# Loading the y tiles of the second output product the way the first product's are loaded, and queueing its weight loads behind them

## The chip, the cores and the metric

The kernel runs on one core of a Trainium2 chip. The metric is the device time of one launch in microseconds (us). Lower is better. The engines are PE (TensorE matmul; its weight loads are shown as PEld), DVE (VectorE), ACT (ScalarE), POOL (GpSimd) and SP (SyncE, which here issues every DMA).

## The reference

One encoder layer is applied to a prompt of 1024 tokens and a sample of 256 tokens, each with 16 meta tokens in front:

```
u = rms_norm(h, norm_w) @ w_in                     # 2048 -> 6656 columns
qa, ka, va, za, qb, kb, vb, zb = split(u)
ya = global_gqa(rope(norm(qa)), rope(norm(ka)), va) * silu(za)              # 8 heads
yb = neighbourhood_attention(norm(qb), norm(kb), vb, rpb) * silu(zb)        # 8 heads
y  = concat([ya, yb]) @ w_out                      # 2048 x 2048
return h + y                                       # without the meta tokens
```

All of it is float32. `neighbourhood_attention` lets each token see a window of 8 rows x 16 columns of a grid that is 64 wide, and the meta tokens.

## The kernel before

A float32 product is made of three matmuls. `split` (L61, L62) writes a rounded copy of a tile with ACT and the remainder with DVE (names ending in `h` and `l`), and PE multiplies h*h, h*l and l*h.

The program has three parts. Two chunks project the tokens strip by strip (`strips`, L210 to L212; tiles `wh`, `wl`, `x`, `xb`, results in `pp`). Attention for the eight global and then the eight windowed heads (called local heads here) is worked into the second chunk. Each local head has four blocks (`attend_strip`): scores on PE (L438 from `qfull` and `kfull`, and L272/L273 from `q` and `km`), maxima and sums with DVE, ACT and POOL (L284, L301), the product with the values (L467, L470 into `po`), and a result `y` that is stored into the DRAM tile `yd` (L319). `yd0` holds the eight global heads and `yd1` the eight local ones. Seven of the local heads run beside the projection; the four blocks of the last one are left for the output product. That head's `qfull` comes by DRAM: the last projection of q is normalized (L237), stored into `q2d` in two pieces (L240), loaded again (L790) and split into `q` (ACT L61, DVE L62).

The output product `outproj` is seven half-size products instead of eight, taken in the order 1, 2, 5, 6, 7, 3, 4, which are called passes here. A pass has five y tiles `t` of 128 tokens from each half, and two column halves `b`, so 10 steps; a step is 24 matmuls into one PSUM tile `pq` (L949 to L951). Steps are numbered n = 0 to 69, y tiles m = n // 2. Pass 1 multiplies `yd0` with w_out rows 0 to 1023, the second pass (number 2) `yd1` with rows 1024 to 2047; both make the same output columns. A pass has 16 weight tiles: `ww` is loaded (L926, L924) into the buffers that held `xb`, and split into `wm`. During the last tile of a pass the weights of the next are split. The four remaining local blocks are woven into steps 3 to 6 by `next(self.blocks)`.

Before the change, `y_load` fills tiles of the pool tag `wl` directly (4 buffers, two for each y tile, one per half of the heads) as long as `self.yr` is None, that is, for pass 1 and for the first tile of pass 2. After `end_attention` has opened the pool `yr` (4 buffers of 512 KB), each later tile of pass 2 is one load into `yr`, which is split from there.

Up to step 10 a scheduler orders the instructions of each engine at build time, by priority (mostly the order in which the program is written) and by its own estimate of when things are ready. From step 10 on, `in_order` chains each engine's instructions in the order written. On the chip each engine then runs its list in that order: an instruction that waits holds up everything behind it on that engine, and a waiting DMA holds up all later DMAs on SP.

Of the kernel before, what the change touches and what calls it, by code (L numbers as in the profile page):

```python
# [12 lines left out]
F32 = mybir.dt.float32  # L13
# [31 lines left out]
WCH = 4  # L45
LAG = 6
TH = (NP + NS) // 2
NT = TH // P
# [6 lines left out]
class Kern:  # L55
# [824 lines left out]
    def y_load(self, p, t):  # L880

        def half(i, h):
            r = self.yr.tile([P, 8, P], F32, tag="yr", name="yr")
            self.nc.sync.dma_start(r[:], self.yd[i][:, NT * h + t])
            return r[:]

        if self.yr is None:
            los = [self.w.tile([P, WCH, P], F32R, tag="wl", name="yl") for _ in range(2)]
            for i, l in enumerate(los):
                self.nc.sync.dma_start(l[:].bitcast(F32), self.yd[p > 1][:, t, WCH * i:WCH * i + WCH])  # L890
            return los
        return [half(*x) for x in {7: [(0, 0), (0, 1)], 5: [(0, 1), (1, 1)], 6: [(0, 0)], 3: [(1, 0)], 2: [(1, 0)], 4: [(1, 1)]}[p]]

    def y_operand(self, p, t, r):
        nc = self.nc
        if len(r[0].shape) == 3 and r[0].shape[1] == WCH:
            his, los, full = [], r, [l[:].bitcast(F32) for l in r]
            for l, f in zip(los, full):
                his.append(self.w.tile([P, WCH, P], F32R, tag="wh", name="yh"))
                self.split(his[-1][:], l[:], f)  # L900
            return his, los
        if p in (2, 4):
            v = r[0]
        elif p == 7:
            v = r[0]
            nc.vector.tensor_tensor(out=v, in0=v, in1=r[1], op=ALU.subtract)
        else:
            v = self.ysum[t][:]
            a, b, op = {5: (r[0], r[-1], ALU.add), 6: (v, r[0], ALU.subtract), 3: (r[0], v, ALU.subtract)}[p]
            nc.vector.tensor_tensor(out=v, in0=a, in1=b, op=op)  # L910
        his, los = [], []
        for i in range(2):
            his.append(self.w.tile([P, WCH, P], F32R, tag="wh", name="yh"))
            los.append(self.w.tile([P, WCH, P], F32R, tag="wl", name="yl"))
            self.split(his[i][:], los[i][:], v[:, WCH * i:WCH * i + WCH])
        return his, los
# [69 lines left out]
        self.nc.sync.dma_start(self.io["y"][:, NT * h + t, FH * c + FB * b:][:, :FB], o[:])  # L986

    def outproj(self, end_attention):
        self.U, self.V, self.yr = {}, {}, None
        order = (1, 2, 5, 6, 7, 3, 4)  # L990
        N = 2 * NT * len(order)

        def step(n):
            q, r = divmod(n, 2 * NT)
            return order[q], *divmod(r, 2)

        def tile_of(m):
            return order[m // NT], m % NT

        M = NT * len(order)  # L1000
        yr, ys, wr, ws, x, out = {}, {}, {}, {}, {}, {}

        def load_y(m):
            if m < M and m not in yr:
                yr[m] = self.y_load(*tile_of(m))

        def make_y(m):
            if m < M:
                load_y(m)
                ys[m] = self.y_operand(*tile_of(m), yr.pop(m))  # L1010

        def load_w(q, j):
            if q < len(order):
                wr[q, j] = self.w_load(order[q], j)

        def make_w(q, j):
            if q < len(order):
                ws[q, j] = self.w_operand(wr.pop((q, j)))

        make_y(0)  # L1020
        for j in range(16):
            load_w(0, j)
            make_w(0, j)
        traced = None
        for n in range(N):
            p, t, b = step(n)
            q, m = n // (2 * NT), n // 2
            if n == 2 * NT - 1:
                for _ in self.blocks:
                    pass  # L1030
            if n == 2 * NT:
                end_attention()
                traced = len(self.nc.cur_bb.bb.instructions)
                load_y(m + 1)
            if n - 2 in out:
                self.store(out.pop(n - 2), *step(n - 2))
            last = t == NT - 1
            if NT - 3 <= t < NT - 1:
                for j in range(4):
                    load_w(q + 1, 8 * (t - NT + 3) + 4 * b + j)  # L1040
            if q:
                for i in (n, n + 1, n + 2):
                    if i < N and i not in x:
                        x[i] = self.x_load(*step(i))
                load_y(m + 2)
            if b == 0 and (q or not last):
                make_y(m + 1)
            if q == 0 and last and b == 1:
                make_y(m + 1)
            ps = self.products([ws[q, 8 * b + k] for k in range(8)], ys[m])  # L1050
            if last:
                for k in range(8):
                    make_w(q + 1, 8 * b + k)
            o = self.out_sums(p, 2 * t + b, ps, x.pop(n, None))
            if o:
                out[n] = o
            if 2 < n < 2 * NT:
                next(self.blocks, None)
            if traced:
                traced = self.in_order(traced)  # L1060
        for n in sorted(out):
            self.store(out[n], *step(n))
# [158 lines left out]
```

## Time and profile before

| | |
|---|---|
| median of 3 runs | 2186.74 us (2185.39 to 2188.92) |
| the profiled execution: its time | 2186.82 us |
| the profiled execution: its span | 2185.0 us |
| mean granted PE clock | 0.996 |
| PE busy | 2158.3 us (99%) |
| DVE, ACT, POOL busy | 1642.2, 1120.7, 519.3 us |
| DMA | 383.83 MB, mean 176 GB/s |

Times in the profile count from the first instruction. A row of the timeline gives the start, the duration, the engine, line, operation and tiles, and in brackets how long the engine was idle before it and what ended that idle time. A matmul's duration is longer than the distance to the next, because matmuls are pipelined; what a matmul costs is that distance. "to landing" of a DMA is the time from its issue until its semaphore says that it is complete.

### The profile page before, as it was taken

The page shows a single profiled execution, that of the slowest core. Times are in us where ns is not written, and L with a number is a line of the kernel's source. Part 1 is how long each engine was busy: PE and PEld are TensorE (multiplying, and loading weights), DVE is VectorE, ACT ScalarE, POOL GpSimd, SP SyncE. Part 2 cuts the span into 40 slices and gives each one's busy share as a digit, 9 for nine tenths or more (in the row PEclk, how much of TensorE's full clock was granted, in tenths as well). Part 3 has the DMA queues.
Part 4 walks back from the last instruction along what each step waited for, and adds up shares of the span by engine and source line. Part 5 has one row for each costly group of instructions (what it writes and reads, how often), then busy time and mean ns, then how long its engine had stood idle before and what let it go on. Part 6 is the DMA issues. An engine that isn't in the chain of part 4 may idle for free.

```text
span 2185.0 us, 34137 instructions
## 1 busy us (share of the span) xinstructions
PE 2158.3 (99%) x11736; PEld 1882.2 (86%) x11736; DVE 1642.2 (75%) x2991; ACT 1120.7 (51%) x2294; POOL 519.3 (24%) x249
## 2 busy tenths in 40 slices
PE   8999999999999999999999999999999999999999
PEld 7888888888888999998999999898989878788887
DVE  7687976787864889996799989777767677545763
ACT  6556544555544666665666666444444454232230
POOL 1232421222211233231133225333223222000000
PEclk9999999999999999999999999999999999999999
DMA  8767899988554333334233334653433471763663
GB/s 295 225 197 229 278 302 313 349 269 263 169 185 142 106 105 110 116 112 143 93 114 109 104 121 158 185 157 132 134 113 123 125 267 37 258 222 110 227 226 106
DMA packets 263038, 383.83 MB, mean 176 GB/s; under 512 B 44976, under 2 KB 113232, under 8 KB 262864
## 3 DMA queue, kind: packets, MB, share of 16 engines
q1 hardware_dynamic: 262864, 381.65, 53.5%
q8 instruction: 92, 1.51, 0.3%
q14 instruction: 82, 0.67, 0.1%
HBM read 281.01 MB, written 100.38 MB: 175 GB/s over the span
## 4 chain that ended last, share of the span: by engine, by line
PE 92%; DVE 3%; DMA 2%; ACT 1%; SPq 1%; issue 1%; POOL 0%; DVEq 0%; ACTq 0%; POOLq 0%
PE pp L210 20%; PE pp L212 20%; PE pp L211 20%; PE pq L949 6%; PE pq L951 6%; PE pq L950 6%; PE sp L438 2%; PE po L470 2%; PE sp L334 1%; PE sp L333 1%; PE sp L332 1%; PE po L372 1%; PE po L373 1%; PE po L374 1%; SPq L227 0%
## 5 line engine op out<-in xcount | busy, mean ns | idle before, releaser
L210 PE MATMUL pp<-x,wh 128*128 128x512 f32 (+1 forms) x1664 | 654.1, 394 | 7.0 <-ACT wh L61 6.5
L212 PE MATMUL pp<-x,wl 128*128 128x512 f32 (+1 forms) x1664 | 649.4, 391 | 0.2 <-DVE wl L62 0.2
L211 PE MATMUL pp<-x,wh 128*128 128x512 f32 (+1 forms) x1664 | 649.4, 391 | 0.0
L210 PEld LDWEIGHTS pp<-x,wh 128*128 128x128 f32 x1664 | 313.3, 188 | 63.7 <-ACT wh L61 7.7
L212 PEld LDWEIGHTS pp<-x,wl 128*128 128x128 f32 x1664 | 313.0, 188 | 62.4 <-DVE wl L62 1.4
L211 PEld LDWEIGHTS pp<-x,wh 128*128 128x128 f32 x1664 | 313.5, 188 | 52.1
L220 POOL PARTITION_ALL_REDUCE m<-ms x78 | 231.8, 2971 | 366.0 <-ACT ms L218 308.1
L62 DVE TENSOR_TENSOR wl<-wr,wh 128x512 fp32r<-128x512 f32 (+1 forms) x290 | 216.5, 749 | 134.0 <-ACT wh L61 109.1
L301 POOL PARTITION_ALL_REDUCE tot<-a x80 | 171.8, 2148 | 487.4 <-DVE a L299 471.2
L61 ACT CAST wh<-wr 128x512 fp32r<-128x512 f32 (+1 forms) x290 | 175.0, 607 | 207.9 <-PE pp L211 185.0
L211 PE MATMUL pp<-xb,wh 128*128 128x272 f32 x832 | 241.8, 291 | 0.0
L210 PE MATMUL pp<-xb,wh 128*128 128x272 f32 x832 | 240.4, 289 | 0.0
L212 PE MATMUL pp<-xb,wl 128*128 128x272 f32 x832 | 239.8, 288 | 0.0
L949 PE MATMUL pq<-wm,yh 128*128 128x512 f32 x560 | 221.1, 395 | 10.1 <-ACT yh L61 5.1
L950 PE MATMUL pq<-wm,yh 128*128 128x512 f32 x560 | 219.7, 392 | 0.0
L951 PE MATMUL pq<-wm,yl 128*128 128x512 f32 x560 | 219.7, 392 | 0.0
L284 POOL PARTITION_ALL_REDUCE ma<-m x80 | 107.2, 1339 | 439.1 <-DVE m L282 427.6
L210 PEld LDWEIGHTS pp<-xb,wh 128*128 128x128 f32 x832 | 157.0, 189 | 7.3
L211 PEld LDWEIGHTS pp<-xb,wh 128*128 128x128 f32 x832 | 156.9, 189 | 7.2
L212 PEld LDWEIGHTS pp<-xb,wl 128*128 128x128 f32 x832 | 157.8, 190 | 0.1
L949 PEld LDWEIGHTS pq<-wm,yh 128*128 128x128 f32 x560 | 106.2, 190 | 32.5 <-ACT yh L61 5.6
L951 PEld LDWEIGHTS pq<-wm,yl 128*128 128x128 f32 x560 | 106.1, 189 | 22.5 <-DVE yl L62 0.2
(207 smaller groups left out, 3838.5 us busy)
## 6 DMA issues: line engine op xcount, KB each, us to landing
wr<-in_w_in SPq DMA_DIRECT2D x414, 256.0 KB, 3.4
wld<-wl SPq DMA_DIRECT2D x132, 256.0 KB, 4.3
wl<-wld SPq DMA_DIRECT2D x132, 256.0 KB, 3.1
yr<-yd SPq DMA_DIRECT2D x39, 512.0 KB, 5.0
wq<-in_w_out SPq DMA_DIRECT2D x64, 256.0 KB, 5.3
td<-wq SPq DMA_DIRECT2D x64, 256.0 KB, 4.4
ww<-td SPq DMA_DIRECT2D x64, 256.0 KB, 5.7
ww<-in_w_out SPq DMA_DIRECT2D x48, 256.0 KB, 5.3
```

The costliest lines, as they stand in the source:

```text
L61: self.hi = nc.scalar.copy(hi, full).ins
L62: return nc.vector.tensor_tensor(out=lo, in0=full, in1=hi.bitcast(F32), op=ALU.subtract).ins
L210: nc.tensor.matmul(p[:, :n], wh[:, k, :], xh[:, :n], start=first, stop=False)
L211: nc.tensor.matmul(p[:, :n], wh[:, k, :], xl[:, :n], start=False, stop=False)
L212: nc.tensor.matmul(p[:, :n], wl[:, k, :], xh[:, :n], start=False, stop=last)
L220: nc.gpsimd.partition_all_reduce(m2[:], ms[:], P, RED.add)
L284: nc.gpsimd.partition_all_reduce(ma[:], m1[:], P, RED.max)
L301: nc.gpsimd.partition_all_reduce(tot[:], a1[:], P, RED.add)
L438: nc.tensor.matmul(dst, k[:, o:o + P], qfv[:, a:e, :], start=True, stop=True)
L949: nc.tensor.matmul(ps[:], yh, wh, start=k == 0, stop=False)
L950: nc.tensor.matmul(ps[:], yh, wl, start=False, stop=False)
L951: nc.tensor.matmul(ps[:], yl, wh, start=False, stop=k == 7)
```

## The change

The second pass is loaded like the first: two loads of 256 KB into `wl` tiles for every y tile (`p in (1, 2)`), with no `yr` tile. In passes 1 and 2 the load of tile m+1 stands in the program at the first step of tile m (b = 0) and its split at the second (b = 1). Before, pass 1 had both at b = 0 (at b = 1 for its last tile), and pass 2 loaded two tiles ahead and split at b = 0. From pass 5 on it is as before, except that the first tile of pass 5 (m = 10) is now loaded where it is split. The loads of the next pass's weights are chained on SP behind the latest direct y load (`issue_after(self.lasty)`). At the start of `outproj` all loads of pass 1 are written ahead of all splits, with the load of the second y tile ahead of the last four weights.

```
     def y_load(self, p, t):
...
-        if self.yr is None:
+        if p in (1, 2):
             los = [self.w.tile([P, WCH, P], F32R, tag="wl", name="yl") for _ in range(2)]
             for i, l in enumerate(los):
-                self.nc.sync.dma_start(l[:].bitcast(F32), self.yd[p > 1][:, t, WCH * i:WCH * i + WCH])
+                self.lasty = self.nc.sync.dma_start(l[:].bitcast(F32), self.yd[p - 1][:, t, WCH * i:WCH * i + WCH]).ins
             return los
...
     def outproj(self, end_attention):
...
+        load_y(0)
+        for j in range(16):
+            if j == 12:
+                load_y(1)
+            load_w(0, j)
         make_y(0)
         for j in range(16):
-            load_w(0, j)
             make_w(0, j)
...
             if n == 2 * NT:
                 end_attention()
                 traced = len(self.nc.cur_bb.bb.instructions)
-                load_y(m + 1)
...
             if NT - 3 <= t < NT - 1:
-                for j in range(4):
-                    load_w(q + 1, 8 * (t - NT + 3) + 4 * b + j)
+                with self.tc.issue_after(self.lasty):
+                    for j in range(4):
+                        load_w(q + 1, 8 * (t - NT + 3) + 4 * b + j)
...
+            direct = m + 1 < 2 * NT
+            if direct:
+                (load_y, make_y)[b](m + 1)
+            elif m + 2 < M:
                 load_y(m + 2)
-            if b == 0 and (q or not last):
-                make_y(m + 1)
-            if q == 0 and last and b == 1:
+            if b == 0 and not direct:
                 make_y(m + 1)
```

The number of instructions is the same on PE, DVE and ACT. Their order differs only from the start of the output product until the second pass, and on SP also before pass 5. Three places follow.

PE where step 0 begins, before: `sp_20203` and `sp_20204` are the scores of the block ahead of the last head's four, `pq_20386` is step 0.

```order
L438 MATMUL sp_20203<-qfull_19454,kfull_19438 128x128 x2
L272 MATMUL sp_20203<-q_19457,km_19442 112x256
L273 MATMUL sp_20203<-q_19457,km_19442 112x256
L438 MATMUL sp_20204<-qfull_19454,kfull_19438 128x192 x2
L949 MATMUL pq_20386<-wm_20298,yh_20290 128x512
L950 MATMUL pq_20386<-wm_20298,yh_20290 128x512
L951 MATMUL pq_20386<-wm_20298,yl_20286 128x512
```

The same place after the change; `qfull_20270`, `kfull_20254` and `q_20273` belong to the last local head, `pq_20380` is step 0.

```order
L438 MATMUL sp_20203<-qfull_19454,kfull_19438 128x128 x2
L272 MATMUL sp_20203<-q_19457,km_19442 112x256
L273 MATMUL sp_20203<-q_19457,km_19442 112x256
L438 MATMUL sp_20204<-qfull_19454,kfull_19438 128x192 x2
L438 MATMUL sp_20504<-qfull_20270,kfull_20254 128x128 x2
L438 MATMUL sp_20505<-qfull_20270,kfull_20254 128x192 x2
L272 MATMUL sp_20504<-q_20273,km_20258 112x256
L273 MATMUL sp_20504<-q_20273,km_20258 112x256
L949 MATMUL pq_20380<-wm_20332,yh_20326 128x512
```

The scores of the last head's first block stood at the end of step 3; they now stand ahead of step 0.

SP around the last head's q, before: `q2d15` is that head's q in DRAM, `ww` here are weights of pass 2.

```order
L926 DMA ww_20741<-in_w_out 128x512
L240 DMA q2d15_164<-rs_r0_20001 128x272
L926 DMA ww_20743<-in_w_out 128x512
L926 DMA ww_20833<-in_w_out 128x512
L478 DMA bt_20268<-in_bt 128x1152
L926 DMA ww_20835<-in_w_out 128x512
L926 DMA ww_20837<-in_w_out 128x512
L926 DMA ww_20839<-in_w_out 128x512
L319 DMA yd1_166<-y_20055 128x4x64
L773 DMA zd15_138<-zt_20181 128x512
L790 DMA qfull_20270<-q2d15_164 128x784
```

The same place after the change; `yl_20315` is the second half of y tile 1.

```order
L890 DMA yl_20315<-yd0_165 128x512
L778 DMA kfull_20254<-kfd9_78 128x240
L779 DMA kfull_20254<-k2d9_148 128x784
L780 DMA kfull_20254<-kfd9_78 128x16
L789 DMA qfull_20270<-qfd15_122 128x240
L240 DMA q2d15_164<-rs_r0_20001 128x272
L790 DMA qfull_20270<-q2d15_164 128x784
L478 DMA bt_20268<-in_bt 128x1152
```

The 16 weight loads of pass 2 are gone from this stretch (they now come between the y loads of tiles 2 to 5), and the load of q follows its store at once.

SP at the end of the last block, before: `y_20829` is that block's result, `yr_21009` the second y tile of pass 2.

```order
L319 DMA yd1_166<-y_20733 128x4x64
L319 DMA yd1_166<-y_20829 128x4x64
L884 DMA yr_21009<-yd1_166 128x1024
L940 DMA o_21011<-in_xr 128x512
L940 DMA o_21013<-in_xr 128x512
L940 DMA o_21015<-in_xr 128x512
L884 DMA yr_21017<-yd1_166 128x1024
```

The same place after the change; `y_20823` is the last block's result, `yl_21015` and `yl_21016` are the halves of the second y tile of pass 2.

```order
L319 DMA yd1_166<-y_20733 128x4x64
L319 DMA yd1_166<-y_20823 128x4x64
L940 DMA o_21009<-in_xr 128x512
L940 DMA o_21011<-in_xr 128x512
L940 DMA o_21013<-in_xr 128x512
L890 DMA yl_21015<-yd1_166 128x512
L890 DMA yl_21016<-yd1_166 128x512
```

The y load has moved behind the three `o` loads, and is in two halves. Of these only the second holds heads of the last block; the first waits for no store, but stands behind it in the list. On PE the last block's value product (L467, L470) stood behind 15 matmuls of step 11 and stands behind 3 now.

More of the change, by code (lines that the diff above doesn't have):

```diff
@@ L885, in half @@
             return r[:]
-        if self.yr is None:
+        if p in (1, 2):
             los = [self.w.tile([P, WCH, P], F32R, tag="wl", name="yl") for _ in range(2)]
             for i, l in enumerate(los):
-                self.nc.sync.dma_start(l[:].bitcast(F32), self.yd[p > 1][:, t, WCH * i:WCH * i + WCH])
+                self.lasty = self.nc.sync.dma_start(l[:].bitcast(F32), self.yd[p - 1][:, t, WCH * i:WCH * i + WCH]).ins
             return los
-        return [half(*x) for x in {7: [(0, 0), (0, 1)], 5: [(0, 1), (1, 1)], 6: [(0, 0)], 3: [(1, 0)], 2: [(1, 0)], 4: [(1, 1)]}[p]]
+        return [half(*x) for x in {7: [(0, 0), (0, 1)], 5: [(0, 1), (1, 1)], 6: [(0, 0)], 3: [(1, 0)], 4: [(1, 1)]}[p]]
     def y_operand(self, p, t, r):
         nc = self.nc
-        if len(r[0].shape) == 3 and r[0].shape[1] == WCH:
+        if p in (1, 2):
             his, los, full = [], r, [l[:].bitcast(F32) for l in r]
@@ L901, in y_operand @@
             return his, los
-        if p in (2, 4):
+        if p == 4:
             v = r[0]
@@ L988, in outproj @@
     def outproj(self, end_attention):
-        self.U, self.V, self.yr = {}, {}, None
+        self.U, self.V = {}, {}
         order = (1, 2, 5, 6, 7, 3, 4)
```

## The prediction

> **What bounds the kernel now.** I read the page first, then PE's waits, then the clock by stretches, then the timeline of PE around the waits.
>
> ```profile
> PE 2158.3 (99%) x11736; PEld 1882.2 (86%) x11736; DVE 1642.2 (75%) x2991; ACT 1120.7 (51%) x2294; POOL 519.3 (24%) x249
> ```
>
> PE is busy for 2158.3 of 2185.0 us, and the change keeps its matmuls. So the time can only move by what PE loses: pauses, and matmuls at a low clock. PE's waits name two long pauses in the part that the change touches:
>
> ```profile
> PE pq L949 <- ACT yh L61: 5.1, 1, 5.1
> PE pq L949 <- DVE z L259: 5.0, 1, 5.0
> ```
>
> The stretches (PE, PEld, DVE, ACT, POOL busy, then granted clock, DMA share, GB/s) show what follows each pause:
>
> ```profile
> 1779.00:1784.00 5.00, 0.02 (x1) 0.03 (x1) 5.00 (x12) 1.26 (x3) 0.00 (x0) 0.85 1.04 373
> 1784.00:1789.50 5.50, 5.50 (x14) 4.34 (x15) 4.10 (x11) 3.31 (x9) 2.01 (x2) 0.52 0.92 301
> 1858.00:1863.30 5.30, 0.19 (x1) 0.00 (x0) 0.00 (x0) 0.65 (x2) 0.00 (x0) 0.78 0.67 214
> 1863.30:1868.00 4.70, 4.68 (x11) 3.64 (x12) 4.52 (x8) 1.63 (x3) 0.00 (x0) 0.52 0.88 307
> ```
>
> After either pause PE runs at half clock for some 5 us. The timeline of PE at the first seam (start of the output product) and at the second (from pass 1 to pass 2):
>
> ```profile
> 1772.76 0.81 PE L438 MATMUL sp<-qfull,kfull 128*128 128x192 f32 x4
> 1773.27 0.53 PE L949 MATMUL pq<-wm,yh 128*128 128x512 f32 x1
> ...
> 1778.64 0.39 PE L951 MATMUL pq<-wm,yl 128*128 128x512 f32 x1
> 1784.01 0.77 PE L949 MATMUL pq<-wm,yh 128*128 128x512 f32 x1 [4.98 <-DVE z L259]
> ...
> 1789.26 0.32 PE L467 MATMUL po<-Pm,vm 128*128 128x256 f32 x1
> ...
> 1854.77 0.28 PE L467 MATMUL po<-Pm,vm 128*128 128x256 f32 x1
> ...
> 1857.80 0.39 PE L951 MATMUL pq<-wm,yl 128*128 128x512 f32 x1
> 1863.32 0.79 PE L949 MATMUL pq<-wm,yh 128*128 128x512 f32 x1 [5.13 <-ACT yh L61]
> ...
> 1868.02 0.40 PE L951 MATMUL pq<-wm,yl 128*128 128x512 f32 x1
> ```
>
> A matmul at full clock costs 0.23 us (24 of step 0 from 1773.27 to 1778.87). First seam: 5.1 us of pause, and the twelve matmuls from 1784.01 to 1789.26 take 5.25 instead of 2.8 us: 7.6 us lost. Second seam: 5.2 us of pause, and the eleven from 1863.32 to 1868.02 take 4.7 instead of 2.5: 7.4 us lost. Together 15.0 us: all that could be won here.
>
> **Second seam: what the change gives.** The rows of the last block's way into y:
>
> ```profile
> 1857.09 0.37 SPq L319 DMA_DIRECT2D yd<-y  x1
> 1859.20 0.33 SPq L884 DMA_DIRECT2D yr<-yd  x1
> 1859.62 1.33 SPq L940 DMA_DIRECT2D o<-in_xr  x3
> ...
> 1862.65 1.14 ACT L61 CAST yh<-yr 128x512 fp32r<-128x512 f32 x2 [7.60 <-DMA yr<-yd]
> yl<-yd SPq DMA_DIRECT2D x12, 256.0 KB, 2.8
> o<-in_xr SPq DMA_DIRECT2D x40, 256.0 KB, 4.1
> ```
>
> Count from the start t of the block's value product (1854.77). Its result is on SP at t + 2.3 and complete at t + 4.4. Before, the load took 3.4, the cast 0.7: step 12 begins at t + 8.6. PE's own end of step 11 was t + 3.2. After the change three `o` loads (1.3) come next, so the first y half is issued at t + 4.1; it lands 2.8 to 4.1 later (a y load, an `o` load; I take 3.6, as the `o` loads are ahead of it), is cast in 0.6, so PE could begin at t + 8.3. The second half is some 0.5 later and has twelve matmuls of cover (2.8 us): no wait. PE itself ends step 11 later, since 21 matmuls follow the product instead of 9: t + 5.9. The pause falls to 2.4 us. It is nothing if the block's result is early, and 5.2 again if it is some 2.8 late; DVE's list there is the same work in both, with the splits of pass 2 around the block.
>
> Does a pause of 2.4 us still cost the clock? The trace has one of about that size, at 610:
>
> ```profile
> 611.26 0.44 PE L253 MATMUL tp<-ident,vt 128*128 128x128 f32 x2 [1.62 <-DVE vm L62]
> 612.21 1.22 PE L210 MATMUL pp<-x,wh 128*128 128x512 f32 x2 [0.51 <-ACT x L158]
> 610.00:612.00 2.00, 0.44 (x2) 0.20 (x2) 1.95 (x6) 0.82 (x3) 0.00 (x0) 0.93 0.78 276
> 612.00:614.00 2.00, 1.79 (x6) 1.60 (x7) 1.81 (x3) 1.04 (x3) 1.06 (x1) 0.50 0.62 175
> ```
>
> Pauses of 1.62 and 0.51 us were enough there, for some 3 us of half clock. I take 1.0 us as the mean of a slow stretch of 3 us (1.5) and of none. The second seam then loses 3.4 instead of 7.4: 4.0 us won, between 0 and 7.4.
>
> The Trainium skill, page "TensorE: Matmul & The Clock Gate", section "HAM oscillation — how this bites in real kernels", gives as a rule that only PE gaps above about 3.4 us cost the clock. By that the 2.4 us pause would be free of it and the sum 1.0 us lower; the 610 rows speak against it, since their two gaps are below 3.4 us.
>
> **First seam: what it costs.** PE runs its list in order, and the scores of the last head's first block now stand ahead of step 0. They need `qfull`, and L272 needs `q` split from it. When is it there?
>
> ```profile
> 1777.08 0.49 DVE L237 SCALAR_TENSOR_TENSOR rs_r<-pp,nqkw,rs_r 128x272 f32<-128x272 f32 x1
> 1783.43 0.43 DVE L259 TENSOR_TENSOR z<-pp,rb 128x272 f32<-128x272 f32 x1
> 1795.02 1.05 ACT L61 CAST q<-qfull 128x1024 fp32r<-128x1024 f32 x1 [3.62 <-DMA qfull<-q2d]
> 1796.10 1.23 DVE L62 TENSOR_TENSOR q<-qfull,q 128x1024 fp32r<-128x1024 f32 x1 [2.83 <-ACT q L61]
> 1781.93 0.33 SPq L240 DMA_DIRECT2D q2d<-rs_r  x1
> 1788.40 0.42 SPq L790 DMA_DIRECT2D qfull<-q2d  x1
> q2d<-rs_r SPq DMA_DIRECT2D x8, 136.0 KB, 1.8
> DMA to landing us min/median/max: 3.3/5.8/6.9
> 1804.16 0.60 PE L438 MATMUL sp<-qfull,kfull 128*128 128x128 f32 x4
> 1805.36 0.53 PE L949 MATMUL pq<-wm,yh 128*128 128x512 f32 x1
> ```
>
> (The landing row is that of L790's eight loads.) DVE's and ACT's lists up to L237 keep their order, so L237 ends at 1777.6 as before. Its store was held on SP until 1781.93, the load until 1788.40, by weight loads, stores and their landings; both are freed now. Store 1.8, load 3.3 to 6.9: I take 3.6, close to the fastest, because the weight loads of pass 2 that kept the DMA at a share of 1.04 are off this stretch. So `qfull` is there at 1783.0, ACT's cast ends at 1784.1, DVE's at 1785.4, the two short products of L272 and L273 and the hand-overs take 0.7: step 0 begins at 1786.1 instead of 1773.27.
>
> Of these 12.8 us, 1.2 are the scores themselves (1804.16 to 1805.36), which fall away later. The pause is 11.6 us where it was 5.1. The low clock follows once, as before: 2.5 us. The wait behind the old pause is covered: z (L259) now stands behind the split of q on DVE and comes at some 1787, while step 1 cannot begin before 1793. So the first seam loses 14.1 instead of 7.6: 6.5 us more. With the fastest load it is 6.2, with the slowest 9.8; 5.5 if the half clock, which began before the scores, ends 1 us sooner.
>
> **The rest.** ACT's `za` (L265) and DVE's sums stand behind the q split and slip by 3 us; their users are the block ahead, whose value product comes at 1795 instead of 1789.26, behind a step that is late itself: nothing. The weight loads of pass 2 come some 20 us later than before, 6 us and more ahead of their casts, which must wait for step 8 anyway: nothing. In pass 2 the y loads wait on SP for `wl` buffers; behind them stand stores and weight loads that are needed a step or more later: nothing. Tile 10's loads move behind tile 11's and behind the store of step 16: four loads of 512 KB at some 370 GB/s are 5.7 us, so tile 10 lands some 8 us after step 16, with its sum and split some 11 us after; step 20 begins 16 us after step 16: nothing, with 3 to 5 us in hand.
>
> **Sum.** +6.5 - 4.0 = +2.5 us. The profiled execution took 2186.82 us, by 0.08 us the median of the runs: 2189.3 us. A measurement of this kernel can tell 0.2% from no change, 4.4 us, so I forecast no change that can be told.
>
> **Rivals.**
> - Slower: the second pause stays. If the last block's result reaches SP about 2.8 us later against PE than I count (its maximum and sums share DVE's list with the 16 weight splits of pass 2, and its product stands 12 matmuls earlier), nothing is won there: +6.5, 2193.3 us. It decides from a gain below 2.1 us on. With a slow `qfull` load it is +9.8, 2196.6. For it: that load's median is 5.8, and it shares the engines with the bias table issued behind it. Against: SP is free at once, and the block's scores stand at the same place, step 7, as before.
> - Faster: the data of the scores is there when PE comes to them, the first seam stays as it is, and the second closes as counted or fully: -4.0 to -7.4, 2182.8 to 2179.4 us. A scheduler that puts the scores there thinks them ready. Against it stands L237 at 1777.08, 3.8 us behind PE's arrival, before a store, a load and a split.
> - The slow clock goes by the skill's rule and the second pause vanishes, with the first as counted: +6.5 - 7.4, 2185.9 us, inside the forecast's case.
>
> **How the numbers follow.** Forecast 0.60 (2185 to 2191), slower rival 0.33, faster rival 0.07. The range 2184.5 to 2194.5 takes in the forecast and the slower rival without its slowest loads; left out are the faster rival and about a third of the slower one. Faster by over 0.2%: 0.07, within: 0.60, slower: 0.33.
>
> **What would show it.** PE's waits should show one pause of 10 to 13 us before the scores of L438 and L272, released by the load of `qfull` and DVE's split of q, none by z, and one of 0 to 3 us before step 12, released by a cast of `yl`. The stretch behind the first should show a clock near 0.5 for about 5 us. A first pause under 8 us, a second of 5 us, or any pause above 1 us in between or behind makes this wrong.

## The result and the profile after

The changed kernel takes 2189.14 us (median of 22 runs, 2186.27 to 2195.86) where the kernel before takes 2186.62 (22 runs, 2183.38 to 2188.92). The ratio is 1.0014, with a 95% interval of 1.0008 to 1.0019: a loss of some 2.5 us, real but smaller than the 0.2% that was set as the bound of no change. The profiled execution took 2188.16 us, with a span of 2186.4.

PE's busy time and its long waits after the change (total us, times, longest):

```profile
PE 2156.9 (99%) x11736; PEld 1880.3 (86%) x11736; DVE 1644.7 (75%) x2991; ACT 1120.0 (51%) x2294; POOL 521.8 (24%) x249
PE sp L438 <- DVE m L452: 9.0, 1, 9.0
PE pq L949 <- ACT yh L61: 3.7, 1, 3.7
```

The wait for z is gone, a wait of 9.0 us ahead of the scores has come, and the second pause has gone from 5.1 to 3.7. The timeline of PE at both seams:

```profile
1772.32 0.81 PE L438 MATMUL sp<-qfull,kfull 128*128 128x192 f32 x4
1782.16 2.47 PE L438 MATMUL sp<-qfull,kfull 128*128 128x128 f32 x8 [9.02 <-DVE m L452]
1784.86 0.63 PE L949 MATMUL pq<-wm,yh 128*128 128x512 f32 x1
1788.20 0.39 PE L949 MATMUL pq<-wm,yh 128*128 128x512 f32 x1
...
1855.03 0.28 PE L467 MATMUL po<-Pm,vm 128*128 128x256 f32 x1
...
1860.79 0.39 PE L951 MATMUL pq<-wm,yl 128*128 128x512 f32 x1
1864.86 0.79 PE L949 MATMUL pq<-wm,yh 128*128 128x512 f32 x1 [3.69 <-ACT yh L61]
1869.17 0.40 PE L949 MATMUL pq<-wm,yh 128*128 128x512 f32 x1
```

Step 0 begins at 1784.86. The row of the pause names L452 on DVE, but what ended it is the load of `qfull`: its landing let ACT's cast start at 1782.10, and PE followed 0.06 us later, as it did in every run with these scores ahead of step 0 (in one of them the row of the pause names that load itself). The way of that q, over all engines:

```profile
1776.65 0.49 DVE L237 SCALAR_TENSOR_TENSOR rs_r<-pp,nqkw,rs_r 128x272 f32<-128x272 f32 x1
1777.16 0.32 SPq L240 DMA_DIRECT2D q2d<-rs_r  x1
1778.90 0.32 SPq L790 DMA_DIRECT2D qfull<-q2d  x1
1782.10 1.04 ACT L61 CAST q<-qfull 128x1024 fp32r<-128x1024 f32 x1 [3.73 <-DMA qfull<-q2d]
1783.18 1.23 DVE L62 TENSOR_TENSOR q<-qfull,q 128x1024 fp32r<-128x1024 f32 x1 [0.79 <-ACT q L61]
1785.13 0.43 DVE L259 TENSOR_TENSOR z<-pp,rb 128x272 f32<-128x272 f32 x1
```

To compare the executions I take three stretches that do the same work: from the last L273 of the block ahead of the last head's (1772.64 before, 1772.20 after) to the start of step 6; from the middle of step 11 to 8 matmuls into step 13 (44 matmuls, 9.98 us without a loss); and steps 20 to 23. Worked out from the starts of PE's matmuls:

| us | before | after | difference |
|---|---|---|---|
| first seam, to step 6 | 47.54 | 50.98 | +3.4 |
| second seam (before: less 1.2 for the value product, which then lay in it) | 17.5 | 15.4 | -2.1 |
| steps 20 to 23 | 21.76 | 22.35 | +0.6 |

That is +1.9. The profiled execution after was 0.4 us ahead when it reached the output product, so its span is 1.4 longer. This start scatters: the profiled executions of all runs reach that L273 between 1768.8 and 1774.2 us. So single executions are compared from there on, and whole times by their medians. A table at the end of the next section has these stretches for the runs on parts of the change.

### The profile page after: what moved, and what is told of

The parts are those of the page before. It is cut to its first block, busy times and chain, and to the rows that moved or that the text cites. A ratio compares the mean times of both kernels' runs of the same rounds, so it can differ in the third digit from the quotient of the medians.

```text
span 2186.4 us, 34153 instructions
## 1 busy us (share of the span) xinstructions
PE 2156.9 (99%) x11736; PEld 1880.3 (86%) x11736; DVE 1644.7 (75%) x2991; ACT 1120.0 (51%) x2294; POOL 521.8 (24%) x249
## 4 chain that ended last, share of the span: by engine, by line
PE 90%; DVE 3%; DMA 3%; ACT 1%; SPq 1%; issue 1%; POOL 1%; POOLq 0%; DVEq 0%; ACTq 0%
PE pp L210 20%; PE pp L212 20%; PE pp L211 20%; PE pq L949 6%; PE pq L951 6%; PE pq L950 6%; PE sp L438 2%; PE po L470 2%; PE sp L334 1%; PE sp L333 1%; PE sp L332 1%; PE po L372 1%; PE po L373 1%; PE po L374 1%; SPq L227 0%
## 5 line engine op out<-in xcount | busy, mean ns | idle before, releaser
L949 PE MATMUL pq<-wm,yh 128*128 128x512 f32 x560 | 219.7, 392 | 3.7 <-ACT yh L61 3.7
L949 PEld LDWEIGHTS pq<-wm,yh 128*128 128x128 f32 x560 | 105.8, 189 | 26.3 <-ACT yh L61 4.5
```

The lines of the kernel that those rows point to most:

```text
L949: nc.tensor.matmul(ps[:], yh, wh, start=k == 0, stop=False)
```

## The experiments

The times of a run stand beside those of the kernel before, run on the same chip. First come the parts of the change apart, then edits of my own.

**The chaining alone** (on the kernel before; a second line, not shown, keeps the latest direct y load in `self.lasty`):

```
-                for j in range(4):
-                    load_w(q + 1, 8 * (t - NT + 3) + 4 * b + j)
+                with self.tc.issue_after(self.lasty):
+                    for j in range(4):
+                        load_w(q + 1, 8 * (t - NT + 3) + 4 * b + j)
```

> The kernel before, with one edit: the loads of the next pass's weights are chained behind the latest direct y load. y of pass 2 is loaded into yr as before. Theory: the chaining alone moves the scores of the last head ahead of step 0 and the last block's value product to step 11+3, so both seams already show what the changed kernel shows: first pause about 9 us before L438 and no pause by z (about 3.4 us lost against before); at the second the load of yr is ready at t + 8.6 after the value product and PE ends step 11 at t + 5.9, a pause of 2 to 3 us, some 3 us won. Sum about 0: 2186 to 2188 us. Rival: the second seam was shortened by the direct loads in halves, not by the order; then its pause of 5 us stays here and only the 3.4 us of the first are added: 2190 us.

2187.82 against 2186.41 us, ratio 1.0004 (0.9995 to 1.0012). Its waits of PE:

```profile
PE sp L438 <- DVE m L452: 8.4, 1, 8.4
PE pq L949 <- ACT yh L61: 3.1, 1, 3.1
```

Both seams are already those of the changed kernel, with the y of pass 2 still in `yr`. The order of PE, the scores ahead of step 0 and the value product at step 11+3, comes from the chaining, and so do the loss at the first seam and the gain at the second. The rival, that the halves shortened the second pause, is out. Why the scheduler moves these places when the loads are chained is not shown.

**The direct loads alone** (on the changed kernel; the chaining above taken back, everything else of the change stays):

> The changed kernel without the chaining of the weight loads; y of pass 2 still goes directly into the wl tiles. Theory: the order of PE is that of before at both seams. First seam as before: two pieces of 5 us and the half clock. Second seam: the first y half, behind three o loads, is cast 9.8 us after the last value product as in the changed kernel (8.6 with yr), while PE ends step 11 at t + 3.2, so the pause is 6 to 7 us instead of 5.2; with the 0.6 us at step 22 about 1.5 to 2 us slower than before: 2188 to 2189 us. Rival: the direct loads in halves shorten the second pause by themselves to about 3.7 us: 2184 to 2185 us.

2188.64 against 2186.41 us, ratio 1.0011 (1.0002 to 1.0020). PE's wait at the first seam, and from the timeline of PE the first matmuls of steps 12 and 22:

```profile
PE pq L949 <- DVE z L259: 5.2, 1, 5.2
```

```profile
1865.00 0.80 PE L949 MATMUL pq<-wm,yh 128*128 128x512 f32 x1 [6.41 <-ACT yh L61]
1922.33 0.50 PE L949 MATMUL pq<-wm,yh 128*128 128x512 f32 x1 [1.00 <-ACT yh L61]
```

As the theory said, with the old order the direct loads make the second pause 6.4 us, longer than the 5.1 before, and step 22 waits another 1.0. In the stretches that is +0.4 at the first seam, +0.8 at the second and +1.6 in steps 20 to 23. So without the chaining the rest of the change is a loss, by these stretches mostly in the steps of the y tiles 10 and 11, of which it loads tile 10 later than before. The other parts of that rest were not run apart.

**The y loads ahead of the `o` loads** (on the changed kernel; the block with `load_y` moved above the one with `x_load`):

> The changed kernel with the y loads of a step written ahead of the three o loads. Theory: issue of the first y half is some 1.3 us earlier, the pause before step 12 falls from 3.7 to about 2.4 us, the rest stays: 1 to 2 us faster than the changed kernel, 2187 to 2188 us. Rival: the y halves are held by the traffic (the o loads now run beside them) and land when they did: 2189 us.

2189.95 against 2186.41 us, ratio 1.0018 (1.0009 to 1.0027): not faster. The time is that of the rival, but both expectations had the mechanism wrong. From the timelines of PE, ACT and DVE:

```profile
1860.71 0.62 ACT L61 CAST yh<-yl 128x512 fp32r<-128x512 f32 x1 [4.93 <-DMA yl<-yd]
1861.38 0.50 PE L949 MATMUL pq<-wm,yh 128*128 128x512 f32 x1 [0.54 <-ACT yh L61]
1862.93 0.69 DVE L959 TENSOR_TENSOR o<-o,u 128x512 f32<-128x512 f32 x1 [5.50 <-DMA o<-in_xr]
1864.26 1.28 DVE L62 TENSOR_TENSOR yl<-yl,yh 128x512 fp32r<-128x512 f32 x2
1865.00 0.80 PE L951 MATMUL pq<-wm,yl 128*128 128x512 f32 x1 [2.88 <-DVE yl L62]
```

The first half did come 3.2 us earlier against the value product, and step 12 began with it. But DVE has the sums of step 10 ahead of the remainder `yl` in its list; they now waited for `o`, and PE stopped two matmuls into the step. The wait changed its name.

**Tile 10 early** (on the changed kernel; tile 11 was loaded two tiles ahead already, so the edit moves only the load of tile 10):

```
-            elif m + 2 < M:
+            if q and m + 2 >= 2 * NT:
                 load_y(m + 2)
```

> The changed kernel with the y tiles 10 and 11 (the first two of pass 5) loaded where the kernel before loads them, two tiles ahead. Theory: tile 11 is there in time and the 0.6 us that step 22 loses in the profile of the changed kernel are gone: 2188.5 us. Rival: the late tiles cost more in most executions than in the profiled one (which was 1 us under the median): 2187.5 us. If they cost nothing that shows: 2189 us.

2189.36 against 2186.41 us, ratio 1.0011 (1.0002 to 1.0020): in the time nothing can be told from the changed kernel. In the profile steps 20 to 23 take 21.76 us again, so the late load of tile 10 is what cost the 0.6; the same execution lost 2.0 more at the second seam than the changed kernel, with a pause of 4.4 us and a longer half clock.

**The scores held behind step 1** (on the changed kernel; L438 and L272/L273 of a block traced at step n issue after the third matmul of step n - 1):

> The changed kernel with only the scores of the last head's blocks held on PE behind step 1 (the scheduler then places the first at step 4). Loads, splits and chaining stay. Theory: the place of the scores alone made the first seam longer, so step 0 starts at once, the pause is that of z again (5 us) and the stretch up to step 6 costs what it cost before, 3.4 us less than in the changed kernel; but the last block's value product is back at step 11+15, and the second pause is 6 to 7 us as with the direct loads alone: 2188 to 2189 us. Rival: the late weight loads and the early q change the first seam by themselves; then the stretch up to step 6 stays within 1 us of the changed kernel's: 2191 us or more.

2192.03 against 2185.68 us, ratio 1.0031 (1.0021 to 1.0042). My theory fell, the rival holds: the first stretch takes 49.97 us, 1.0 less than in the changed kernel and 2.4 more than before. Two rows of DVE's timeline, PE's longest wait at the seam and the wait behind it say why:

```profile
1782.38 1.23 DVE L62 TENSOR_TENSOR q<-qfull,q 128x1024 fp32r<-128x1024 f32 x1 [0.80 <-ACT q L61]
1784.32 0.44 DVE L259 TENSOR_TENSOR z<-pp,rb 128x272 f32<-128x272 f32 x1
```

```profile
PE pq L955 <- DVE z L259: 6.5, 1, 6.5
```

```profile
1789.87 0.36 PE L468 MATMUL po<-Pm,vm 128*128 128x256 f32 x1 [1.64 <-DVE Pm L294]
```

(L955 is L949 there, L468 is L467.) With q early, its split stands ahead of z on DVE, and step 1 waits 6.5 us for z where it waited 5; then the value product of the block ahead waits 1.6 us, which it did not before. So with the scores out of the way 2.4 of the 3.4 us are still lost: DVE's list does it too, where z and the sums stand behind whatever DVE waits for.

**z early** (on the kernel before; `z_scale` holds L259, which `z_evac` had inside, so line numbers behind it shift by up to 5):

```
+                zs = [self.z_scale(p, o, n) for p, (o, n) in zip(ps, BL)]
-                for p, (o, n) in zip(ps, BL):
+                for p, (o, n), z in zip(ps, BL, zs):
                     zt = self.ev.tile([P, n], F32, tag="ev", name="zt")
-                    self.z_evac(p, o, n, [(0, n, zt[:])])
+                    self.z_evac(p, o, n, [(0, n, zt[:])], z)
...
```

> The kernel before, with one edit: of a late z projection both pieces are scaled out of PSUM (L259) ahead of the rest of their chains, so that the second PSUM tile comes free at once. Theory: the first seam of the kernel before is only the wait for that tile; step 1 then follows step 0 without a pause, DVE's last weight split for step 1 ends some 1 us after step 0, and with the pause of 5 us the half clock goes: 6 to 7.5 us faster than before, 2179 to 2180.5 us. The second seam keeps its 5 us. Rival: another wait is right behind (weights or y still being split on DVE), over 2 us, which costs the clock too: 2183 us or more.

2181.50 against 2187.99 us, ratio 0.9971 (0.9960 to 0.9982). The wait for z is gone, with no other right behind it; at 1789.40 a new one stands, of the value product of the block ahead (L471 is L467, L298 is L294). Its row of PE's timeline, and the windows of the pause and of the low clock:

```profile
1789.40 0.55 PE L471 MATMUL po<-Pm,vm 128*128 128x256 f32 x1 [2.32 <-DVE Pm L298]
```

```profile
1787.10:1789.20 2.10, 0.00 (x0) 0.00 (x0) 1.77 (x5) 1.59 (x4) 0.00 (x0) 1.00 1.02 265
1789.20:1792.60 3.40, 3.20 (x11) 3.13 (x12) 0.47 (x2) 0.85 (x3) 1.79 (x1) 0.51 0.88 304
```

So theory and rival each hold in part: the 6.5 us won lie in the theory's 6 to 7.5, and a wait of over 2 us, not the one that the rival named, has come in and cost the clock. The profiled execution is the slowest of the seven (2183.86 us). Its first stretch takes 43.94 us, 3.6 less than before; it does not show where the rest of the median's 6.5 was won.

**Blocks one step earlier** (on the chaining alone: `if 1 < n` for `if 2 < n` ahead of `next(self.blocks)`):

> The kernel before with the weight loads chained behind y (as in the run of the chaining alone) and the four last local blocks woven in one step earlier. Theory: the last block's value product then stands at step 9+19, some 8 us of PE work earlier, so its y is there long before step 12: no second pause and no half clock there, 7.5 us; the first seam stays as with the chaining alone, 3.4 us worse than before. Sum about -4: 2182 to 2183 us. Rival: the blocks, one step earlier, wait themselves (POOL's and DVE's sums between their scores and value products do not come earlier), and PE stops in front of a value product instead: 2185 us or more.

2182.61 against 2187.99 us, ratio 0.9976 (0.9965 to 0.9987). The second stretch takes 9.98 us: no pause and no low clock. The first holds one block more and takes 53.15 us, so about what it takes with the chaining alone (50.68, and some 2.3 for a block's scores and value product).

**All three, and the same on the direct loads:**

> The kernel before with three edits: weight loads chained behind y, z scaled early, blocks one step earlier; y of pass 2 still through yr. With these the scores of the last head stand behind step 2, when q has been there for some 5 us. Theory: both seams close, of the 15 us lost at them 13 to 15 are won: 2171.5 to 2174 us. Rival: the scores at step 3 still wait for q, or a value product for its sums, some 3 us with the half clock behind it: 2177 us.

> The changed kernel with the same two edits (z early, blocks one step earlier) and y tiles 10 and 11 loaded two tiles ahead. Theory: once no step waits for y of the last block, it makes no difference whether pass 2 loads y directly or through yr: the same 2171.5 to 2174 us as the run beside it, within 1 us. Rival: the direct loads, which wait on SP for wl tiles with stores and weight loads behind them, cost by themselves: 2 us or more slower than the run beside it.

2177.36 and 2176.36 against 2187.99 us, ratios 0.9949 (0.9936 to 0.9961) and 0.9946 (0.9933 to 0.9958). The two medians do not differ by more than the runs scatter, so the rival's 2 us do not show in the time. But in the profile the direct loads still cost something: PE waits for the cast of y ahead of step 12 there, and the second stretch takes 11.47 us, where it is 9.97 with `yr`:

```profile
PE pq L954 <- ACT yh L61: 1.0, 1, 1.0
```

They won 10.6 and 11.6 us where the theory said 13 to 15. The reason is the rival's value product; its row and the window behind it in the run with `yr`:

```profile
1792.33 0.55 PE L471 MATMUL po<-Pm,vm 128*128 128x256 f32 x1 [3.65 <-DVE Pm L298]
```

```profile
1792.30:1797.40 5.10, 5.08 (x16) 4.52 (x17) 3.20 (x6) 2.35 (x5) 1.79 (x1) 0.50 0.80 279
```

**That value product held behind 9 matmuls of step 3** (on the run with `yr`; `pv0` is its first matmul, the lines that keep it and the step's number are not shown):

```
+            if (self.step, k) == (3, 2):
+                self.tc.add_manual_dep(self.pv0, mm.name, mybir.DependencyInfo(
+                    mybir.DependencyClass.NoSync, mybir.DependencyReason.DATA), reason="pv")
```

> As the run with chaining, early z and early blocks, and with the value product of the block ahead of the last head held behind the first 9 matmuls of step 3 (it stood at step 2+15, where PE waited 3.65 us for its sums and then ran at half clock for 5 us). Theory: the pause and the low clock behind it, about 6 us together, are gone, and no other pause over 1 us is left between the start of the output product and its end: 2171 to 2173 us. Rival: later blocks, which share one PSUM tile for their value products with this one, are pushed and stop PE in its place: 2176 us.

2168.79 against 2185.68 us, ratio 0.9921 (0.9908 to 0.9933): 16.9 us faster than the kernel before, and better than both kernels and than I expected. One window over nearly the whole output product, in this run and in the kernel before:

```profile
1765.00:2165.00 400.00, 398.20 (x1804) 331.86 (x1802) 243.72 (x408) 128.08 (x244) 19.58 (x11) 1.00 0.55 189
```

```profile
1765.00:2180.00 415.00, 404.89 (x1818) 336.83 (x1817) 245.30 (x412) 130.20 (x247) 20.18 (x11) 0.98 0.54 184
```

PE is busy for all but 1.8 of 400 us, at full clock (before: all but 10.1 of 415, at 0.98). The profiled execution is 18.0 us shorter, of which 2.8 were ahead of the output product. The 15.2 left agree with the 15.0 us that the prediction read off the two seams as all that could be won there; the median's 16.9 has an interval of 14.6 to 20.1.

The three stretches in the runs on parts of the change (us):

| run | to step 6 | second seam | steps 20 to 23 |
|---|---|---|---|
| chaining alone | 50.68 | 15.26 | 21.76 |
| direct loads alone | 47.95 | 18.3 (less 1.2) | 23.34 |
| y ahead of `o` | 50.70 | 16.60 | 23.00 |
| tile 10 early | 51.02 | 17.41 | 21.76 |
| scores held | 49.97 | 18.8 (less 1.2) | 23.86 |

## Why the prediction came out right, step by step

The forecast of 2189.3 us met 2189.14, and the forecast's case held: more lost at the first seam than won at the second. But its terms were both too large and erred against each other: +6.5 was +3.4, -4.0 was -2.1, and a "nothing" was +0.6. So the direction and the two mechanisms were right, and that the number is met within 0.2 us is luck.

Of the signs that the prediction named, the releasers came as named, z released no pause, and no pause above 1 us came in between or behind. The first pause was 9.0 us, below the 10 to 13 named and above the 8 that would have made it wrong; the second was 3.7 where 0 to 3 were named. Behind the first, PE worked 3.8 us at half clock where about 5 were named.

**First seam, the q chain: right, 0.8 us too long.** L237 was not held, the store and the load followed at once, and q was split before step 0. Predicted was a start of step 0 12.8 us later; counted from the scores ahead of it, it was 12.0 (11.59, and 0.44 by which this execution was ahead). The load landed in 3.2 us (1778.90 to 1782.10) where 3.6 was taken.

**First seam, "the low clock follows once, as before: 2.5 us": wrong, this is the term that failed.** The stretches of low clock after the change:

```profile
1773.20:1775.80 2.60, 0.00 (x0) 0.00 (x0) 2.60 (x7) 2.58 (x7) 0.00 (x0) 1.00 0.92 329
1775.80:1786.00 10.20, 3.84 (x13) 3.64 (x14) 9.41 (x21) 4.94 (x10) 0.00 (x0) 0.50 0.43 143
1786.00:1788.00 2.00, 2.00 (x10) 1.58 (x10) 2.00 (x6) 1.42 (x5) 1.06 (x1) 0.98 0.34 131
```

The clock fell during the pause and PE took up work at 1782.16 with the first scores, which ran at half clock while q was still being split, so that cost little. At 1786.00, 1.1 us into step 0, it was back: step 0's first 12 matmuls took 3.34 us instead of 2.87 in the kernel before. Half a microsecond, not 2.5: that is most of the difference between +6.5 and +3.4, and the 0.8 of the q chain nearly all of the rest. The loss that is left is the late start of step 0: 12.0 us, less 1.2 for the scores, which fall away later. The prediction did name a half clock that ends sooner, but priced 1 us of it at 1.0; at half rate it is 0.5.

**z covered: right.** L259 came at 1785.13, and step 1 had no wait.

**Second seam, "PE could begin at t + 8.3": it was t + 9.8.** The rows of SP and ACT:

```profile
1857.82 0.37 SPq L319 DMA_DIRECT2D yd<-y  x1
1858.28 1.41 SPq L940 DMA_DIRECT2D o<-in_xr  x3
1859.74 0.91 SPq L890 DMA_DIRECT2D yl<-yd  x2
1864.19 0.62 ACT L61 CAST yh<-yl 128x512 fp32r<-128x512 f32 x1 [8.05 <-DMA yl<-yd]
```

The store came at t + 2.8 instead of 2.3, the first half was issued at t + 4.7 instead of 4.1, and it took 4.4 us to land where 3.6 was taken, with three `o` loads in front of it and the other half behind. PE did end step 11 later as counted (t + 6.0, predicted 5.9). So the pause was 3.7 and not 2.4, and the half clock behind it cost 1.6 (in the last section, a row shows 3.14 us of PE at half rate) and not 1.0: together 1.9 less won. The prediction credited the gain to both the order and the loads; the runs show the order as its only source.

**"Tile 10 ... nothing, with 3 to 5 us in hand": wrong, it cost 0.6 here and 1.2 to 2.1 in three runs of the same loads.** The rows of DVE, after the change:

```profile
1903.55 1.23 DVE L910 TENSOR_TENSOR ysum<-yr 128x1024 f32<-128x1024 f32 x1 [3.55 <-DMA yr<-yd]
1911.57 0.68 DVE L959 TENSOR_TENSOR o<-o,u 128x512 f32<-128x512 f32 x1
1912.89 4.90 DVE L62 TENSOR_TENSOR wm<-ww,wm 128x512 fp32r<-128x512 f32 x8
1917.71 0.69 DVE L959 TENSOR_TENSOR o<-o,u 128x512 f32<-128x512 f32 x1
1919.03 1.22 DVE L910 TENSOR_TENSOR ysum<-yr 128x1024 f32<-128x1024 f32 x1
```

And the sums of tiles 10 and 11 before:

```profile
1898.99 1.22 DVE L910 TENSOR_TENSOR ysum<-yr 128x1024 f32<-128x1024 f32 x1
1914.47 1.22 DVE L910 TENSOR_TENSOR ysum<-yr 128x1024 f32<-128x1024 f32 x1
```

Tile 10 itself was in time: step 20 began without a wait. But its sum, 4.6 us later than before, waits on DVE, and behind it stand the splits of eight weights for each of the last two steps of a pass. Their period on DVE is 6.14 us (1911.57 to 1917.71), longer than the 5.4 of a step on PE, so nothing was made up, and tile 11's sum at the end of the list came 4.6 us later than before as well, just too late for step 22. I had counted the cover of the tile that waits, not that of what stands behind it.

**Rivals.** The slower one ("the second pause stays") did not happen: y of the last block was 1.5 us late, where some 2.8 were needed. The faster one is out: PE did reach the scores 9 us ahead of their data. The third, by the Trainium skill's rule, is out too: the low clock came back behind the second pause, and that pause did not vanish. At 3.7 us it is too long to test the rule itself, which is weighed below.

## What to carry to other kernels

An edit that only chains DMAs can move the order of a busy engine far from the place it was written for; compare the order of every engine before counting what the edit itself costs. Where a wait is taken away or moved, follow the list of each in-order engine behind the waiting instruction: three times here (z behind the q split, `yl` behind the `o` sums, tile 11 behind tile 10) the loss lay with what stood behind. The time was in two seams that held 15 us, and closing them took small edits to the order (free the PSUM tile first, start the last blocks a step earlier, hold one product back), not faster loads.

## What the runs showed of the hardware

The low clock came in stretches of about 3.4, 6.8 and 10.2 us: 3.4 with early z (rows above), 10.2 at the first seam of the changed kernel (row above), 3.4 at its second (first row below), and 6.8 twice in the kernel before (second and third row):

```profile
1864.60:1868.00 3.40, 3.14 (x7) 2.44 (x8) 2.70 (x5) 0.82 (x2) 0.00 (x0) 0.50 0.82 290
1782.60:1789.40 6.80, 5.39 (x13) 4.27 (x14) 5.50 (x15) 3.42 (x9) 1.91 (x2) 0.51 0.94 308
1861.00:1867.80 6.80, 4.48 (x11) 3.47 (x12) 4.32 (x7) 2.23 (x4) 0.00 (x0) 0.50 0.93 334
```

Within one execution all ends of these stretches lie on one grid: from the end of the first to the start of the second it is 71.6 us in the kernel before, 21 times 3.41, and 78.6 in the changed kernel, 23 times that to 0.2 us; in the six other runs with two such stretches it is 20 to 23 times that. So a stretch does not end a fixed time after PE takes up work: at the first seam it was 5.4 us before (1784.01 to 1789.4) and 3.8 after the change (1782.16 to 1786.0), most of which the scores took up.

The Trainium skill, page "TensorE: Matmul & The Clock Gate", section "Part 1: The HAM clock gate", tells of a free-running window of about 3.4 us that does not start with the work; the lengths and the grid agree with that. It would explain why the low clock behind the second pause cost 1.6 us in the changed kernel, 2.0 with the chaining alone and 2.9 with tile 10 early, with the same order of PE there (each is what the stretch takes beyond 9.98, less the pause from start to start of PE's matmuls). The rule that the Trainium skill gives on that page, section "HAM oscillation — how this bites in real kernels", to have no PE gaps above about 3.4 us, is not enough here: 2.3 us without a matmul, from 1787.1 to 1789.4, brought a low stretch of 3.4 us. How much of a window PE must be busy to keep the clock, or to get it back, was not tried.
